# Seven block products for eight on all 2048 output columns in two quarters of an MLP, with four of the products moved into the first projection

## The chip, the cores and the metric

The kernel runs on one core of a Trainium2 chip. The metric is device microseconds per execution; lower is better. The kernel before takes 2056.1 us, the median of three runs (2055.78 to 2056.94).

The engines go by the profile's names: PE is TensorE (matmuls), PEld its weight loads, DVE is VectorE, ACT is ScalarE, POOL is GpSimd, and SP is the queue that issues nearly all DMAs.

## What is computed

One layer of a transformer trunk in float32 on 256 tokens of width 2048: a mixer of retention and gated DeltaNet, a cross-attention, a squared-ReLU MLP with a hidden width of 8192, and a final RMSNorm. The change touches the MLP alone:

```python
h = rms_norm(x, norm_ffn_g[l])
x = x + jnp.square(jax.nn.relu(h @ w_ff1[l])) @ w_ff2[l]
...
return rms_norm(x, norm_final_g)
```

`w_ff1` is 2048 x 8192 and `w_ff2` is 8192 x 2048. Both are read from HBM once.

## The kernel before

**Products of split operands.** Every float32 operand of a matmul is split into a high part, rounded by a cast on ACT (`whi`, line 125), and the remainder, a subtraction on DVE (`wlo`, line 126). A product of two split matrices is three matmuls: high x high, high x low, low x high. Weights come in fetches of 1 MiB (`fetch`, line 104) into one of three `raw` buffers, and are split in two halves of 128 x 1024. The split halves lie in `whi`/`wlo` (three buffers each), and every fourth half in `whx`/`wlx` (`half_tiles`), so that four halves are alive at a time: the cast of a half can start when PE is done with the half four before it.

**The MLP** runs in four quarters (`fb`, line 1258), each of 2048 hidden columns.

- *First projection* of a quarter: eight calls of `blocks` (line 221), each 256 hidden columns, with the weights stationary. A block takes two fetches, that is four halves. It ends in PSUM in the `s0`/`s1` tiles; ACT copies one part out (line 217), DVE adds the other (218), and `evac_h` (line 1266) squares the ReLU on DVE (1267), casts the high part on ACT (1269) and subtracts the low part on DVE (1270) into the quads `hid`.
- *Second projection* of a quarter: 256 tokens x 2048 hidden rows times 2048 x 2048 of `w_ff2`. The output columns are four groups of 512, `n` = 0 to 3; the hidden rows are four quads of 512, `q` = 0 to 3. `plain(n, q)` (line 1187) fetches one 512 x 512 piece and does 24 matmuls (four rows of blocks, two token halves, three matmuls). `add` (line 1135) adds a finished PSUM tile into the result on DVE.

**Seven for eight.** Hidden rows 0 to 1023 of a quarter (`q` = 0, 1) times columns 0 to 1023 (`n` = 0, 1) are a product of 2 x 2 blocks: the tokens in halves, the hidden rows in even and odd strips of 128, the columns in two groups of 512. `with_seven` (line 1156) does it in the seven products of Strassen's scheme in Winograd's form. A `product` (line 1196) is one token half times one block: 12 matmuls. It casts and subtracts a block's halves (lines 1202 and 1203), and, where `then` is given, forms the next difference of blocks on DVE (1207, two subtractions of 128 x 1024). The four blocks `b11`, `b12`, `b22`, `b21` lie in `rt` and `tr`, a 1 MiB block in each half, loaded by `load_block` (line 1164). The sums of the token side are made on DVE and ACT during the first projection (`token_sums`, line 1146). Some products go into several output tiles, and so `add` reads one PSUM tile twice. The rest (`n` = 2, 3 in all rows, `n` = 0, 1 in the second half of the rows) is `plain`: 12 of these and seven products make a quarter's second projection.

**What sets the order.** The program is written as one stream; a scheduler then orders each engine's instructions by priority. Fetches, casts and splits have a high priority and run ahead as far as buffers let them. Two orders are pinned in the code: `triple` (line 1179) puts each matmul of the second projection after the last one of the step before (`ends`), and `add_later` (line 1141) puts an `add` after the last split that was recorded so far. PSUM has two pairs `s0`/`s1` and four banks `b`; `shared` and `p5` are two of the banks, and `shared` holds one product after another: a product that starts in it must wait until DVE has added the one before into the result.

Of the kernel before, what the change touches and what calls it, by code (L numbers as in the profile page):

```python
# [14 lines left out]
ALU = mybir.AluOpType  # L15
# [37 lines left out]
def trunk(ctx: ExitStack, tc: tile.TileContext, x_f, mem_f, positions, lead_f, small_f, w_in, ret_gn_g, w_out, w_xq,  # L53
# [41 lines left out]
    def step():  # L95
        if steps and next(steps[0], steps) is steps:
            steps.pop(0)
# [91 lines left out]
    def cols(w, c0, n=512):  # L189
        return lambda q: [(0, w[q * 512:(q + 1) * 512, c0:c0 + n])]  # L190

    def blocks_in_steps(quads, w, c0, nb, evac):

        k = 16 // nb
        ps = stream_ps()
        n = nb * P
        for g in range(KT // k):  # L200
            halves = fetch([(0, w[g * k * P:(g + 1) * k * P, c0:c0 + n])], k, n, at=AT_BLOCKS)
            for i in range(k):
                kk = g * k + i
                xh, xhl = quads[kk // 4][0][:, kk % 4, :], quads[kk // 4].both[:, kk % 4, :]
                wh, wl = halves[i // (k // 2)]
                for b in range(nb):
                    bs = slice(b * P, (b + 1) * P)
                    lh, ll = wh[:, i % (k // 2), bs], wl[:, i % (k // 2), bs]
                    pe.matmul(ps[b], lh, xhl, start=kk == 0, stop=False)  # L209
                    pe.matmul(ps[b][:, :S], ll, xh, start=False, stop=kk == KT - 1)  # L210
                if i % (k // 2) == k // 2 - 1:
                    step()
                    yield
        for b in range(nb):
            with tc.high_priority(offset=50000):
                o = sm.tile([P, S], F32, name="bo", tag="bo", bufs=2)
                act.activation(o, ps[b][:, S:], AF.Copy)  # L217
                vec.tensor_add(o, o, ps[b][:, :S])  # L218
                evac(b, o)
# [936 lines left out]
    def with_seven(hid, rows, last):  # L1156


        own = [stream_ps() for _ in range(2)]
        shared, p5 = bank(), bank()  # L1160
        own += [[bank(), bank()]] * 2
        opened, ends, reads = set(), [], []

        def load_block(to, which, n):

# [47 lines left out]
        def part(b, t):  # L1213
            return lambda i: [a[:, 2 * (i % 2) + b, t * P:(t + 1) * P] for a in hid[i // 2]]
# [1 line left out]
        def summed(j):  # L1216
            return lambda i: [a[:, i, j * P:(j + 1) * P] for a in s_hl]

        first = 2 if last else 3
        plain(first, 0)  # L1220
        load_block(b11, 0, 0)
        plain(first, 1)
        load_block(b12, 0, 1)
        product(shared, part(0, 0), b11, "shared", (b11, b12, b11))
        read((0, 0, shared))
        plain(first, 2)
        load_block(b22, 1, 1)
        product(p5, summed(0), b11, "p5", (b11, b22, b11))
        read((1, 0, p5), (1, 1, p5))
        plain(0, 2)  # L1230
        product(own[1][0], summed(3), b22, (1, 0), (b12, b22, b12))
        plain(first, 3)
        load_block(b21, 1, 0)
        read(*((first, t, own[first][t]) for t in range(NT)))
        product(shared, summed(1), b11, "shared", (b11, b21, b11))
        read((1, 0, shared))
        plain(0, 3)
        product(own[0][0], part(1, 0), b21, (0, 0))
        read((0, 0, own[0][0]))
        if not last:  # L1240
            plain(2, 0)
        plain(1, 2)
        product(shared, summed(2), b12, "shared")
        read((0, 1, shared), (1, 1, shared))
        if not last:
            plain(2, 1)
        product(own[0][1], part(1, 1), b11, (0, 1))
        read((0, 1, own[0][1]))
        if not last:
            plain(2, 2)  # L1250
            plain(2, 3)
            read(*((2, t, own[2][t]) for t in range(NT)))
        plain(1, 3)
        read(*((1, t, own[1][t]) for t in range(NT)))
        for those in reads:
            add(*those)

    for fb in range(4):
        hid = []
        rows = w_ff2[0, fb * D:(fb + 1) * D, :]  # L1260
        for b2 in range(8):
            hs = fp.tile([P, 2, S], F32, name="hs", tag="hs", bufs=2)
            if b2 % 2 == 0:
                hid.append(quad_a())

            def evac_h(b, ps):
                vec.scalar_tensor_tensor(hs[:, b, :], ps, 0.0, ps, op0=ALU.max, op1=ALU.mult)
                qh, ql = (a[:, b2 % 2 * 2 + b, :] for a in hid[-1])
                act.activation(qh, hs[:, b, :], AF.Copy)
                vec.tensor_sub(ql, hs[:, b, :], qh.bitcast(F32))  # L1270
# [97 lines left out]
```

## Time and profile before

| | |
|---|---|
| median of three runs | 2056.1 us |
| profiled execution, its own time | 2056.91 us |
| its span, first to last instruction | 2055.2 us |
| PE busy | 2043.9 us, 99% of the span |
| DVE busy | 1511.4 us, 74% |
| ACT busy | 1130.3 us, 55% |
| second quarter of the MLP: first projection | 1527.99 to 1616.17 us |
| second quarter of the MLP: second projection | 1616.17 to 1700.52 us |
| third quarter: first and second projection | from 1700.52 and from 1788.70 to 1873.06 us |

A group's line gives the source line, the engine, the operation, what it writes and reads, the shape and the count; behind the bar its busy time and the mean of one in ns; behind the second bar the idle time of its engine just before it and what ended most of it. A row of the timeline starts with the start and the duration in us. In a table by windows each engine has its busy time and, in brackets, its count of instructions.

### The profile page before, as it was taken

The numbers are of one execution on the slowest core, as the hardware profiler recorded it, in microseconds if no ns is written. First come the engines' busy times: TensorE is split into PE (matmuls) and PEld (weight loads), VectorE is DVE, ScalarE is ACT, GpSimd is POOL, SyncE is SP. The second block draws the span as 40 slices with busy tenths as digits, with TensorE's granted clock in tenths as the row PEclk, the third lists the DMA queues.
The fourth block names the chain that finished last, engine by engine and source line by source line (L and its number), as shares of the span: only waits on it lengthen the run. The fifth ranks groups of instructions, "written<-read, shape, count | busy, mean of one in ns | idle before, by whom it ended". The sixth has DMA issues, their size and how long they took to land.

```text
span 2055.2 us, 28469 instructions
## 1 busy us (share of the span) xinstructions
PE 2043.9 (99%) x10874; PEld 1759.8 (86%) x10874; DVE 1511.4 (74%) x2409; ACT 1130.3 (55%) x1827; POOL 36.4 (2%) x50
## 2 busy tenths in 40 slices
PE   9999999999999999999999999999999999999998
PEld 7888888988888888888888899888888888888887
DVE  5887788779667875888567665777867777686785
ACT  5665764575457555755455565655545445454554
POOL 0000000000000000000000000000000000000000
PEclk9999999999999999999999999999999999999999
DMA  9689556456555655555467665569556646736662
GB/s 327 204 258 299 183 185 198 155 189 202 178 168 186 200 180 165 191 190 172 164 216 232 189 188 159 182 180 263 196 184 187 243 154 195 266 124 196 221 217 104
DMA packets 329225, 405.24 MB, mean 197 GB/s; under 512 B 34928, under 2 KB 239360, under 8 KB 328960
## 3 DMA queue, kind: packets, MB, share of 16 engines
q1 hardware_dynamic: 328656, 402.74, 60.8%
q8 instruction: 85, 1.39, 0.3%
q10 hardware_dynamic: 432, 0.69, 0.1%
q14 instruction: 52, 0.43, 0.1%
HBM read 389.74 MB, written 11.55 MB: 195 GB/s over the span
## 4 chain that ended last, share of the span: by engine, by line
PE 96%; DVE 1%; DMA 1%; issue 1%; ACT 1%; SPq 0%; POOLq 0%; POOL 0%; DVEq 0%; ACTq 0%
PE s L209 33%; PE s L210 17%; PE b L1182 9%; PE s L167 8%; PE s L168 8%; PE s L166 8%; PE s L1182 5%; PE s L399 1%; PE s L398 1%; PE s L400 1%; PE b L793 1%; PE b L826 1%; PE b L138 0%; DMA raw<-w_ff 0%; PE b L137 0%
## 5 line engine op out<-in xcount | busy, mean ns | idle before, releaser
L126 DVE TENSOR_TENSOR wlo<-raw,whi 128x1024 fp32r<-128x1024 f32 x610 | 744.9, 1222 | 344.2 <-ACT whi L125 338.2
L209 PE MATMUL s<-q,whi 128*128 128x512 f32 x2816 | 975.0, 391 | 0.8 <-DVE bo L218 0.6
L125 ACT ACTIVATE whi<-raw 128x1024 fp32r<-128x1024 f32 x610 | 646.3, 1060 | 574.9 <-PE s L209 204.1
L210 PE MATMUL s<-q,wlo 128*128 128x256 f32 x2816 | 771.8, 281 | 0.4 <-DVE wlo L126 0.3
L209 PEld LDWEIGHTS s<-q,whi 128*128 128x128 f32 x2816 | 521.1, 188 | 105.0 <-DVE bo L218 0.9
L210 PEld LDWEIGHTS s<-q,wlo 128*128 128x128 f32 x2816 | 528.9, 188 | 11.5 <-DVE wlo L126 1.2
L167 PE MATMUL s<-wlo,q 128*128 128x512 f32 x716 | 281.7, 393 | 0.0
L168 PE MATMUL s<-whi,q 128*128 128x512 f32 x716 | 279.4, 390 | 0.0
L166 PE MATMUL s<-whi,q 128*128 128x512 f32 x716 | 258.9, 390 | 0.0
L166 PEld LDWEIGHTS s<-whi,q 128*128 128x128 f32 x716 | 134.3, 188 | 28.0
L168 PEld LDWEIGHTS s<-whi,q 128*128 128x128 f32 x716 | 134.6, 188 | 27.0
L167 PEld LDWEIGHTS s<-wlo,q 128*128 128x128 f32 x716 | 134.6, 188 | 26.7
L217 ACT ACTIVATE bo<-s 128x256 f32<-128x256 f32 x192 | 72.9, 380 | 108.2 <-PE s L210 108.1
L218 DVE TENSOR_TENSOR bo<-bo,s 128x256 f32<-128x256 f32 x192 | 79.9, 416 | 54.0 <-ACT bo L217 53.7
L1182 PE MATMUL b<-whi,q 128*128 128x512 f32 x360 | 114.7, 389 | 0.0
L209 PE MATMUL s<-q,whx 128*128 128x512 f32 x256 | 89.4, 389 | 0.0
L126 DVE TENSOR_TENSOR wlx<-raw,whx 128x1024 fp32r<-128x1024 f32 x54 | 66.0, 1222 | 28.1 <-ACT whx L125 27.2
L125 ACT ACTIVATE whx<-raw 128x1024 fp32r<-128x1024 f32 x54 | 57.2, 1060 | 52.5 <-PE s L209 23.0
L1182 PE MATMUL s<-whi,q 128*128 128x512 f32 x248 | 79.8, 389 | 0.0
L1182 PEld LDWEIGHTS b<-whi,q 128*128 128x128 f32 x360 | 67.6, 188 | 14.1
L210 PE MATMUL s<-q,wlx 128*128 128x256 f32 x256 | 71.2, 280 | 0.0
L1182 PE MATMUL b<-wlo,q 128*128 128x512 f32 x180 | 70.1, 389 | 0.0
(383 smaller groups left out, 2186.0 us busy)
## 6 DMA issues: line engine op xcount, KB each, us to landing
raw<-w_in SPq DMA_DIRECT2D x143, 1024.0 KB
raw<-w_ff SPq DMA_DIRECT2D x112, 1024.0 KB
raw<-w_xkv SPq DMA_DIRECT2D x29, 1024.0 KB
raw<-w_out SPq DMA_DIRECT2D x16, 1024.0 KB
raw<-w_xq SPq DMA_DIRECT2D x16, 1024.0 KB
raw<-w_xo SPq DMA_DIRECT2D x16, 1024.0 KB
rt<-w_ff SPq DMA_DIRECT2D x8, 1024.0 KB
tr<-w_ff SPq DMA_DIRECT2D x8, 1024.0 KB
```

Of the source, the lines that this page charges most:

```text
L125: latest["hi"] = act.activation(hi[:, cs], src[:, cs], AF.Copy).ins
L126: latest["lo"] = vec.tensor_sub(lo[:, cs], src[:, cs], hi[:, cs].bitcast(F32)).ins
L166: pe.matmul(o, xh, wh, start=first, stop=False)
L167: pe.matmul(o, xh, wl, start=False, stop=False)
L168: pe.matmul(o, xl, wh, start=False, stop=last)
L209: pe.matmul(ps[b], lh, xhl, start=kk == 0, stop=False)
L210: pe.matmul(ps[b][:, :S], ll, xh, start=False, stop=kk == KT - 1)
L217: act.activation(o, ps[b][:, S:], AF.Copy)
L218: vec.tensor_add(o, o, ps[b][:, :S])
L398: pe.matmul(o, xh, wh, start=kk == 0 and c0 == 0, stop=False)
L399: pe.matmul(o, xh, wl, start=False, stop=False)
L1182: ins = pe.matmul(o, lhs[l], rhs[r], start=key not in opened, stop=last and j == 2, skip_group_check=True).ins
```

## The change

The second and third quarter (`fb` 1 and 2, called *early* in the code) do the seven products on columns 1024 to 2047 as well, and begin with the first unit's products during the first projection. The first and the fourth quarter are as before.

- Per early quarter 8 `plain` and 14 products replace 12 `plain` and 7 products.
- `with_seven` becomes a generator. In an early quarter the first block is loaded after the fourth block of the first projection, and then after each of the last four of the eight blocks one product is done: `part(0, 0)`, `summed(0)`, `summed(1)`, `summed(2)`. The matmuls of the first projection are pinned behind these (`ends`).
- The other three products of the first unit, the 8 `plain` and the seven products of the second unit follow. The second unit's blocks are loaded into the same four places of `rt` and `tr` as these come free.
- In the last four blocks of an early quarter's first projection the squared ReLU is no longer one instruction on DVE but two on ACT (`Relu`, then `Square`).

```diff
@@ blocks_in_steps
-                    pe.matmul(ps[b], lh, xhl, start=kk == 0, stop=False)
-                    pe.matmul(ps[b][:, :S], ll, xh, start=False, stop=kk == KT - 1)
+                    with tc.issue_after(ends[-1]) if ends else ExitStack():
+                        pe.matmul(ps[b], lh, xhl, start=kk == 0, stop=False)
+                        ins = pe.matmul(ps[b][:, :S], ll, xh, start=False, stop=kk == KT - 1).ins
                 if i % (k // 2) == k // 2 - 1:
+                    if ends is not None:
+                        ends.append(ins)
@@ with_seven
+        if early:
+            load_block(b11, 0, 0)
+            yield
+            load_block(b12, 0, 1)
+            product(shared, part(0, 0), b11, "shared", (b11, b12, b11))
+            read((0, 0, shared))
+            yield
+            load_block(b22, 1, 1)
+            product(p5, summed(0), b11, "p5", (b11, b22, b11))
+            read((1, 0, p5), (1, 1, p5))
+            yield
+            load_block(b21, 1, 0)
+            product(shared, summed(1), b11, "shared", (b12, b22, b12))
+            read((1, 0, shared))
+            yield
+            product(shared, summed(2), b12, "shared", (b11, b21, b11))
+            read((0, 1, shared), (1, 1, shared))
+            yield
+            for n in range(2):
+                take(n, stream_ps())
+            plain(0, 2)
+            load_block(b12, 0, 3)
+            product(own[1][0], summed(3), b22, (1, 0))
+            plain(0, 3)
+            load_block(b22, 1, 3)
+            product(own[0][0], part(1, 0), b21, (0, 0))
+            read((0, 0, own[0][0]))
+            product(own[0][1], part(1, 1), b11, (0, 1))
+            read((0, 1, own[0][1]))
+            plain(1, 2)
+            load_block(b11, 0, 2)
+            take(2, [bank(), bank()])
+            plain(2, 2)
+            load_block(b21, 1, 2)
+            opened.difference_update(("shared", "p5"))
+            product(shared, part(0, 0), b11, "shared", (b11, b12, b11))
+            read((2, 0, shared))
+            plain(1, 3)
+            read(*((1, t, own[1][t]) for t in range(NT)))
+            product(p5, summed(0), b11, "p5", (b11, b22, b11))
+            read((3, 0, p5), (3, 1, p5))
+            plain(2, 3)
+            take(3, stream_ps())
+            product(own[3][0], summed(3), b22, (3, 0), (b12, b22, b12))
+            plain(3, 2)
+            product(shared, summed(1), b11, "shared", (b11, b21, b11))
+            read((3, 0, shared))
+            plain(3, 3)
+            read(*((3, t, own[3][t]) for t in range(NT)))
+            product(own[2][0], part(1, 0), b21, (2, 0))
+            read((2, 0, own[2][0]))
+            product(shared, summed(2), b12, "shared")
+            read((2, 1, shared), (3, 1, shared))
+            product(own[2][1], part(1, 1), b11, (2, 1))
+            read((2, 1, own[2][1]))
+        else:
...
@@ evac_h and the loop
+                if early and b2 > 3:
+                    act.activation(ps, ps, AF.Relu)
+                    act.activation(hs[:, b, :], ps, AF.Square)
+                else:
+                    vec.scalar_tensor_tensor(hs[:, b, :], ps, 0.0, ps, op0=ALU.max, op1=ALU.mult)
...
-            blocks(h3, w_ff1[0], fb * D + b2 * 256, 2, evac_h)
+            blocks(h3, w_ff1[0], fb * D + b2 * 256, 2, evac_h, ends if early else None)
+            if early and b2 > 2:
+                next(parts_of)
...
-        with_seven(hid, rows, fb == 3)
+        for _ in parts_of:
+            pass
```

Where the instructions stand after the scheduler shows in the built programs. The source lines shift: 218 becomes 221, 1138 becomes 1141, 1203 becomes 1206, 1207 becomes 1210, 1267 becomes 1341, 1269 becomes 1343, 1270 becomes 1344; 1338 and 1339 are the new ReLU and square. Names keep their buffer numbers here.

**DVE ahead of the end of the first projection's last block.** Before, in the second quarter, the splits of that block's second fetch (`raw_15223`) stand between the steps of the evacuation of the seventh block (`s0_15080`, `s1_15081`), and the splits of the first `plain` step (`raw_15285`) follow:

```order
L126 TENSOR_TENSOR wlo_15226<-raw_15223,whi_15225 128x1024
L218 TENSOR_TENSOR bo_15166<-bo_15166,s0_15080 128x256
L1267 SCALAR_TENSOR_TENSOR hs_15078<-bo_15166 128x256
L126 TENSOR_TENSOR wlo_15230<-raw_15223,whi_15229 128x1024
L218 TENSOR_TENSOR bo_15172<-bo_15172,s1_15081 128x256
L1270 TENSOR_TENSOR q_15079<-hs_15078,q_15079 128x256
L1267 SCALAR_TENSOR_TENSOR hs_15078<-bo_15172 128x256
L126 TENSOR_TENSOR wlo_15288<-raw_15285,whi_15287 128x1024
L1270 TENSOR_TENSOR q_15079<-hs_15078,q_15079 128x256
L126 TENSOR_TENSOR wlx_15292<-raw_15285,whx_15291 128x1024
```

Now, in the same quarter, the splits of the last block's second fetch (`raw_15304`) are followed by the end of the seventh block's evacuation, the splits of the fourth product (`whi_15360`, `whi_15364`), two differences of blocks, and the addition of `b_14879`, the `shared` bank with the third product in it, into which the fourth product is to go:

```order
L126 TENSOR_TENSOR wlo_15307<-raw_15304,whi_15306 128x1024
L126 TENSOR_TENSOR wlx_15311<-raw_15304,whx_15310 128x1024
L1344 TENSOR_TENSOR q_15133<-hs_15132,q_15133 128x256 x2
L1206 TENSOR_TENSOR wlo_15361<-rt_10152,whi_15360 128x1024
L1206 TENSOR_TENSOR wlo_15365<-rt_10152,whi_15364 128x1024
L1210 TENSOR_TENSOR rt_10152<-tr_13007,rt_10152 128x1024 x2
L1141 SCALAR_TENSOR_TENSOR res_13006<-b_14879,rstd3q_13000,res_13006 128x512
L126 TENSOR_TENSOR wlo_15390<-raw_15387,whi_15389 128x1024
```

The square of the ReLU has left DVE here, and a product's two splits, two differences and one addition have come in; the addition stands behind the differences.

**DVE in the second projection, where a difference is formed.** Before, in the second quarter, one product with its differences is followed by a fetched step (`raw_15552`) and two additions of one finished `plain` column group:

```order
L1203 TENSOR_TENSOR wlo_15529<-rt_10152,whi_15528 128x1024
L1203 TENSOR_TENSOR wlx_15533<-rt_10152,whx_15532 128x1024
L1207 TENSOR_TENSOR rt_10152<-tr_13007,rt_10152 128x1024 x2
L126 TENSOR_TENSOR wlo_15555<-raw_15552,whi_15554 128x1024
L1138 SCALAR_TENSOR_TENSOR res_13006<-b_15283,rstd3q_13000,res_13006 128x512
L1138 SCALAR_TENSOR_TENSOR res_13006<-b_15284,rstd3q_13000,res_13006 128x512
L126 TENSOR_TENSOR wlo_15559<-raw_15552,whi_15558 128x1024
```

Now, around the product `summed(3)` of the second unit (`whi_15712`, `whi_15716`), with `raw_15674` being `plain(2, 3)` and `raw_15734` being `plain(3, 2)`:

```order
L1141 SCALAR_TENSOR_TENSOR res_13006<-s0_15385,rstd3q_13000,res_13006 128x512
L1141 SCALAR_TENSOR_TENSOR res_13006<-s1_15386,rstd3q_13000,res_13006 128x512
L126 TENSOR_TENSOR wlx_15681<-raw_15674,whx_15680 128x1024
L1206 TENSOR_TENSOR wlo_15713<-tr_13007,whi_15712 128x1024
L1141 SCALAR_TENSOR_TENSOR res_13006<-b_14880,rstd3q_13000,res_13006 128x512 x2
L1206 TENSOR_TENSOR wlo_15717<-tr_13007,whi_15716 128x1024
L1210 TENSOR_TENSOR rt_10152<-tr_13007,rt_10152 128x1024 x2
L126 TENSOR_TENSOR wlo_15737<-raw_15734,whi_15736 128x1024
```

Four additions and two differences now stand between the splits of three steps.

**ACT at the evacuation of the seventh block.** Before, its PSUM tiles are copied out (`bo_15166`, `bo_15172`) between casts, and the high part of `q` is cast when DVE has squared:

```order
L217 ACTIVATE bo_15166<-s0_15080 128x256
L125 ACTIVATE whi_15229<-raw_15223 128x1024
L217 ACTIVATE bo_15172<-s1_15081 128x256
L1269 ACTIVATE q_15079<-hs_15078 128x256
L125 ACTIVATE whi_15287<-raw_15285 128x1024
L1269 ACTIVATE q_15079<-hs_15078 128x256
L125 ACTIVATE whx_15291<-raw_15285 128x1024
```

Now the same block (`bo_15220`, `bo_15227`):

```order
L220 ACTIVATE bo_15220<-s0_15134 128x256
L125 ACTIVATE whi_15268<-raw_15262 128x1024
L220 ACTIVATE bo_15227<-s1_15135 128x256
L125 ACTIVATE whi_15306<-raw_15304 128x1024
L1338 ACTIVATE bo_15220<-bo_15220 128x256
L125 ACTIVATE whx_15310<-raw_15304 128x1024
L1339 ACTIVATE hs_15132<-bo_15220 128x256
L1338 ACTIVATE bo_15227<-bo_15227 128x256
L1343 ACTIVATE q_15133<-hs_15132 128x256
L1339 ACTIVATE hs_15132<-bo_15227 128x256
L1343 ACTIVATE q_15133<-hs_15132 128x256
L1205 ACTIVATE whi_15360<-rt_10152 128x1024
```

Each ReLU waits for DVE's line 221 and stands in ACT's queue ahead of the cast of a later weight half (`whx_15310`).

More of the change, by code (lines that the diff above doesn't have):

```diff
@@ L1154, in token_sums, with with_seven @@
         split([a[:, i, :] for a in s_hl], sv.rearrange("p a s -> p (a s)"))
-    def with_seven(hid, rows, last):
-        own = [stream_ps() for _ in range(2)]
+    def with_seven(hid, rows, last, early):
+        own = {}
         shared, p5 = bank(), bank()
-        own += [[bank(), bank()]] * 2
-        opened, ends, reads = set(), [], []
+        opened, reads = set(), []
         def load_block(to, which, n):
@@ L1217, in summed @@
             return lambda i: [a[:, i, j * P:(j + 1) * P] for a in s_hl]
[L1219 to L1246, printed above, removed]
@@ L1255, in with_seven @@
         for those in reads:
             add(*those)
+    ends = []
     for fb in range(4):
@@ L1260, in trunk @@
         rows = w_ff2[0, fb * D:(fb + 1) * D, :]
+        early = fb in (1, 2)
+        parts_of = with_seven(hid, rows, fb == 3, early)
+        ends.clear()
         for b2 in range(8):
```

49 lines of the change are left out of this document (41 added, 8 removed).

## The prediction, on record before the run

> **What bounds the kernel now.** I read the page's busy times and its chain of work that ended last, then the MLP by windows, then what PE waited for there.
>
> ```profile
> PE 2043.9 (99%) x10874; PEld 1759.8 (86%) x10874; DVE 1511.4 (74%) x2409; ACT 1130.3 (55%) x1827; POOL 36.4 (2%) x50
> ...
> PE 96%; DVE 1%; DMA 1%; issue 1%; ACT 1%; SPq 0%; POOLq 0%; POOL 0%; DVEq 0%; ACTq 0%
> ```
> ```profile
> 1380.00:2015.00 635.00, 635.00 (x3261) 544.84 (x3260) 473.79 (x610) 322.65 (x406) 0.00 (x0) 1.00 0.64 204
> ```
> ```profile
> 1527.99:1616.17 88.18, 88.18 (x514) 78.16 (x512) 61.57 (x96) 44.34 (x65) 0.00 (x0) 1.00 0.71 228
> 1616.17:1700.52 84.35, 84.35 (x374) 69.82 (x373) 64.71 (x65) 41.38 (x42) 0.00 (x0) 1.00 0.49 161
> ```
> ```profile
> PE s L1182 <- DVE wlo L1203: 0.3, 1, 0.3
> PE s L1182 <- DVE wlo L126: 0.2, 1, 0.2
> ```
>
> The chain is PE for 96%. In the window from 1380 to 2015 us PE is busy for every one of 635.00 us, at a granted clock of 1.00; the two other windows are the second quarter's projections. The last rows are all the waits of PE from 1380 us to the end: two, both near the end. So here time is the number of matmuls times their spacing, as long as nobody makes PE wait; DVE (64.71 of 84.35 us) and ACT are hidden.
>
> **What is removed.** The count of the second projection's matmuls alone gives their spacing:
>
> ```profile
> 1616.17:1700.52 84.35, 84.35 (x372) 69.64 (x372) 1.00 0.49 161
> ```
>
> That is 84.35 / 372 = 0.2267 us. The order of the two programs has 1392 matmuls of line 1182 before and 1368 after (line 1185 there): 24 fewer, 12 per early quarter, or **24 x 0.2267 = 5.44 us**. The blocks of the first projection keep their 256 pairs of matmuls (88.18 / 8 = 11.02 us a block, 2.755 us for one of its four halves). Outside the two quarters the orders of all engines are the same. So the question is what of 5.44 us comes back as waits of PE.
>
> **What DVE and ACT get.** The costs:
>
> ```profile
> L126 DVE TENSOR_TENSOR wlo<-raw,whi 128x1024 fp32r<-128x1024 f32 x610 | 744.9, 1222 | 344.2 <-ACT whi L125 338.2 <-PE b L698 0.5
> L125 ACT ACTIVATE whi<-raw 128x1024 fp32r<-128x1024 f32 x610 | 646.3, 1060 | 574.9 <-PE s L209 204.1 <-PE s L168 171.0 <-PE b L1182 52.8
> L218 DVE TENSOR_TENSOR bo<-bo,s 128x256 f32<-128x256 f32 x192 | 79.9, 416 | 54.0 <-ACT bo L217 53.7
> L217 ACT ACTIVATE bo<-s 128x256 f32<-128x256 f32 x192 | 72.9, 380 | 108.2 <-PE s L210 108.1
> ...
> L1207 DVE TENSOR_TENSOR rt<-tr,rt 128x1024 f32<-128x1024 f32 x24 | 28.2, 1217 | 0.0
> L1138 DVE SCALAR_TENSOR_TENSOR res<-b,rstd3q,res 128x512 f32<-128x512 f32 (+1 forms) x39 | 27.5, 736 | 1.5 <-PE b L168 1.5
> L1267 DVE SCALAR_TENSOR_TENSOR hs<-bo 128x256 f32<-128x256 f32 x64 | 26.9, 421 | 1.1
> L1270 DVE TENSOR_TENSOR q<-hs,q 128x256 fp32r<-128x256 f32 x64 | 26.7, 418 | 0.0
> L1269 ACT ACTIVATE q<-hs 128x256 fp32r<-128x256 f32 x64 | 26.0, 407 | 2.8 <-DVE hs L1267 2.8
> ```
>
> Queued behind one another, DVE's instructions start closer than they last:
>
> ```profile
> 1639.03 1.40 DVE L1138 SCALAR_TENSOR_TENSOR res<-b,rstd3q,res 128x512 f32<-128x512 f32 x2
> 1640.35 1.22 DVE L1203 TENSOR_TENSOR wlx<-tr,whx 128x1024 fp32r<-128x1024 f32 x1
> 1641.48 2.35 DVE L1207 TENSOR_TENSOR rt<-tr,rt 128x1024 f32<-128x1024 f32 x2
> 1643.76 2.35 DVE L126 TENSOR_TENSOR wlo<-raw,whi 128x1024 fp32r<-128x1024 f32 x2
> 1646.05 1.23 DVE L1203 TENSOR_TENSOR wlo<-rt,whi 128x1024 fp32r<-128x1024 f32 x1
> ```
>
> So an addition takes 1.32 / 2 = 0.66 us, a difference 1.14, a split 1.14.
>
> A *round* (a block, then a product) gives PE 11.02 + 12 x 0.2267 = 13.74 us. DVE has six splits (6.84), two differences (2.28), up to two additions (1.32) and four small steps of 0.42 (1.68): 12.1 us. ACT has six casts (6.36), two copies (0.76), two casts of `q` (0.81) and four new steps, priced as that cast (1.63): 9.6 us. The rest of the second projection, 8 `plain` and 10 products, gives PE 8 x 5.44 + 10 x 2.72 = 70.7 us; DVE has 36 splits (41.0), 8 differences (9.1), 16 additions (10.6) and two small steps: 61.5 us. Both fit, at 88% and 87%, against 77% of the second projection now. What can fail is a single place. I follow the running sum there.
>
> ```profile
> 1610.66 0.39 PE L209 MATMUL s<-q,whi 128*128 128x512 f32 x1
> ...
> 1610.80 1.06 ACT L125 ACTIVATE whx<-raw 128x1024 fp32r<-128x1024 f32 x1 [1.40 <-PE s L209]
> ```
> ```profile
> 1611.90 1.23 DVE L126 TENSOR_TENSOR wlx<-raw,whx 128x1024 fp32r<-128x1024 f32 x1 [1.21 <-ACT whx L125]
> ```
> ```profile
> 2016.40 1.22 DVE L1203 TENSOR_TENSOR wlo<-rt,whi 128x1024 fp32r<-128x1024 f32 x1
> ...
> 2017.68 0.50 PE L1182 MATMUL s<-wlo,q 128*128 128x512 f32 x1 [0.27 <-DVE wlo L1203]
> ```
>
> PE leaves a half at 1610.66; its buffer's next cast starts 0.14 us later, the split 1.10 us after that. In the last pair PE starts 0.06 us after the split it waited for ends (2017.62), and its matmul takes 0.50 us for 0.39, so a wait costs some 0.11 us beside itself.
>
> *The fourth product (new wait on the bank `shared`).* It starts when the eighth block ends, and must wait for the addition of the third product, which stands on DVE behind the fourth product's second split and two differences. That split's buffer comes free when the block is half done, two halves or 5.51 us earlier. The chain: 0.14 + 1.10 + 1.14 + 2.28 + 0.74 (the addition) + 0.06 = 5.46 us. It fits by 0.05 us, less than I can tell. Behind this matmul stands all of PE. Nothing at best, some 0.2 us if it misses; I take 0.15 a quarter, **0.3 us**.
>
> *The plain step (3, 2).* From the first split of the second `p5` product, which waits for its cast 2.6 us after the product ahead of it has started, DVE has six splits, four differences and five additions before the first split of (3, 2) starts: 6.84 + 4.56 + 3.30 = 14.7 us; with that split it is ready at 2.6 + 14.7 + 1.2 = 18.5 us. PE needs it after three products and two plain steps, 19.0 us. Cover 0.5 us: cost nothing, or up to 0.9 if the sixteen instructions follow at their durations (0.08 us more each).
>
> *The three products in a row at the end* give PE 8.16 us, DVE six splits and four additions, 9.5 us; but two of the splits are done before PE arrives, and the splits come out at least 1.2 us ahead. Nothing.
>
> *Evacuation on ACT.* The square's two steps are needed by `plain(0, 3)`, which starts 10.9 us after the last block: hidden. Were ACT late, the cover gone would be a whole cast and split.
>
> *DMA.* A quarter still loads 16 MiB for each projection. Four blocks beside eight fetches in 70.7 us make 12.6 MB, 178 GB/s, and a round's 3 MiB in 13.74 us 229 GB/s, while a stretch before ran at
>
> ```profile
> 1598.50:1617.00 18.50, 18.50 (x108) 16.38 (x107) 11.22 (x16) 8.51 (x12) 0.00 (x0) 1.00 1.03 382
> ```
>
> without making PE wait. The reload that SP can issue last, of the second unit's `b11`, waits for the first unit's seventh product's splits; it has some 11 us until its own cast must be done. At 382 GB/s 1 MiB takes 2.7 us. Nothing.
>
> **The sum.** The profiled execution took 2056.91 us, 1.71 around its span of 2055.2. 2056.91 - 5.44 + 0.3 = 2051.8; the median of the runs is 0.8 lower, so **2051.0 us**.
>
> **The rivals.**
>
> *DVE's backlog reaches PE.* Against it: the five rows above, 10 us of DVE without a gap, and no wait of PE. For it: both waits at the end are for a split. If instructions follow at their durations, the fourth product waits 0.3, (3, 2) 0.8, each with 0.1 for the restart: 1.2 a quarter; with 0.06 us between them as well, some 2.0. That gives back 2.4 to 4.0: **2053.4 to 2055.0 us**. It decides from 0.05 us at the first place.
>
> *ACT's queue behind the new ReLU (slower).* The ReLU waits for DVE's line 221, and a weight half's cast stands behind it, whose split DVE needs for PE: two first-in-first-out engines in a loop. When the loop closes, a round loses a cast and a split, 1.06 + 1.22 = 2.28 us; in all eight rounds 18.2: **2069 us**; slower than before by over 0.2% from five of the eight. It needs line 221 to be late by over 5 us: by the sums DVE reaches it 2 us after a block's product starts, ACT passes the cast 4.5 us after, and PE needs the split at 11.0. The idle time of 53.7 us behind line 217 in 192 evacuations, 0.28 each, speaks against it.
>
> *The longer evacuation itself.* Two steps of 0.41 us on ACT stand for one of 0.42 on DVE. Were each on PE's path, the 16 evacuations would cost 16 x 0.4 = 6.5 us: **2057.5 us**. Against it stand the 10.9 us above. The rows make the two engines' steps alike, and DVE the fuller engine. The Trainium skill, ScalarE: Activation LUTs, section Rules for kernel authors, advises VectorE and not ScalarE for a ReLU. By that rule this part of the change loses time, up to the 6.5 us; the trace bears it out only where the steps are waited for. No table is loaded for the new steps: the two programs hold five loads each, one of which lasts
>
> ```profile
> L253 ACT ACT_TABLE_LOAD  x1: 1283/1283/1283, 1.2 to 1.2; - x1
> ```
>
> *The change doesn't do what it says.* Then PE's count would not fall; the order shows that it does. A chance remains that PE loses as much in the strict order of blocks and products: **2056 us**.
>
> **How the numbers follow.** A measurement tells about 0.2% from no change, 4.1 us: faster is under 2052.0. My forecast, with at most 1 us of waits, has 0.62; DVE's backlog 0.22, within 0.2%; the queue behind the ReLU 0.09, slower; the longer evacuation 0.05 and no effect 0.02, both within. So faster 0.62, same 0.29, slower 0.09. The range goes from no wait and a low run, 2050.3, to the end of the backlog, 2055.0, which holds the first two cases (0.84).
>
> **What would show it.** In the second and third quarter 360 matmuls of the second projection's kind each for 372, 0.227 us apart; PE busy throughout both but for a gap of 0.1 to 0.2 us ahead of each quarter's fourth product, released by DVE's addition. A gap at (3, 2) released by a split would be the backlog; gaps inside the blocks, released by a cast, ACT's queue. The forecast is wrong if the sum of PE's gaps in the two quarters is over 1.4 us.

## The result, and the profile after

The kernel with the change takes 2051.68 us (median, 2049.37 to 2052.57), the kernel before 2056.14 us beside it (2054.61 to 2056.95): a ratio of 0.9978, with a 95% interval of 0.9969 to 0.9987. That is 4.5 us less, 2.7 to 6.4 by the interval. The profiled execution of the changed kernel took 2050.97 us for a span of 2049.2.

Two more lines have moved: 209 and 210 in the blocks are now 210 and 211, and 1182 in the products is 1185.

The page of the changed kernel, its busy times and the shares of its chain:

```profile
PE 2038.1 (99%) x10850; PEld 1756.6 (86%) x10850; DVE 1542.9 (75%) x2433; ACT 1153.2 (56%) x1871; POOL 36.3 (2%) x50
...
PE 96%; DMA 1%; DVE 1%; issue 1%; ACT 1%; SPq 0%; POOLq 0%; POOL 0%; DVEq 0%; ACTq 0%
```

PE has 24 instructions fewer (10874 before), DVE 24 and ACT 44 more, and the chain is PE for 96% as before. All that PE waited for from 1380 us to the end of the changed kernel (line, releaser, us in total, times, longest):

```profile
PE s L1185 <- DVE wlo L1206: 0.2, 1, 0.2
PE s L1185 <- DVE wlo L126: 0.2, 1, 0.2
```

These are the same two waits near the end as before; the two changed quarters have none that the view counts. To compare them I take the stretch from the first block of the second quarter to the first product of the fourth. First before, then after (length; busy time of PE, PEld, DVE, ACT, POOL with instructions; granted clock; DMA share; GB/s):

```profile
1527.99:1961.23 433.24, 433.24 (x2281) 374.12 (x2280) 314.14 (x416) 215.79 (x277) 0.00 (x0) 1.00 0.62 202
```
```profile
1526.80:1955.26 428.46, 428.46 (x2258) 369.70 (x2256) 345.01 (x440) 238.34 (x321) 0.00 (x0) 1.00 0.63 204
...
1581.91:1623.33 41.42, 41.42 (x230) 36.05 (x229) 34.88 (x41) 26.28 (x43) 0.00 (x0) 1.00 0.58 191
```

The stretch is 4.78 us shorter; the forecast was 5.14, and 24 matmuls alone would be 5.44. (The last row is its first three rounds of a product and a block.) The rest of the difference between the two profiled executions, 5.94 - 4.78 = 1.16 us, lies outside the change: in the MLP's first block, the first matmul behind those of the norm starts at 1362.40 us in place of 1363.65, behind code that is the same. In the five profiles below that leave the code ahead of it alone, this matmul starts between 1362.71 and 1364.75 us. So whole executions can be compared only to a microsecond or two; stretches of the same code, as the runs below show, agree to a few hundredths.

The place that the prediction named, around the second quarter's fourth product:

```profile
1617.90 1.06 ACT L1205 ACTIVATE whi<-rt 128x1024 fp32r<-128x1024 f32 x1 [1.68 <-PE s L210]
...
1618.99 1.23 DVE L1206 TENSOR_TENSOR wlo<-rt,whi 128x1024 fp32r<-128x1024 f32 x1 [1.51 <-ACT whi L1205]
...
1620.14 2.35 DVE L1210 TENSOR_TENSOR rt<-tr,rt 128x1024 f32<-128x1024 f32 x2
...
1622.41 0.74 DVE L1141 SCALAR_TENSOR_TENSOR res<-b,rstd3q,res 128x512 f32<-128x512 f32 x1
...
1623.33 0.43 PE L1185 MATMUL b<-whi,sh 128*128 128x512 f32 x1
...
1623.61 0.40 PE L1185 MATMUL b<-wlo,sh 128*128 128x512 f32 x1
```

Cast, split, two differences and addition stand behind one another as in the forecast's chain, and the matmul starts 0.18 us after the addition. It lasts 0.43 us for 0.40, and the second one follows 0.28 us behind it, where 0.233 is usual at such a place: some 0.05 us are lost, too little for the list of waits.

### The profile page after: what moved, and what is told of

The parts are those of the page before. It is cut to its first block, busy times and chain, and to the rows that moved or that the text cites. A ratio compares the mean times of both kernels' runs of the same rounds, so it can differ in the third digit from the quotient of the medians.

```text
span 2049.2 us, 28493 instructions
## 1 busy us (share of the span) xinstructions
PE 2038.1 (99%) x10850; PEld 1756.6 (86%) x10850; DVE 1542.9 (75%) x2433; ACT 1153.2 (56%) x1871; POOL 36.3 (2%) x50
## 4 chain that ended last, share of the span: by engine, by line
PE 96%; DMA 1%; DVE 1%; issue 1%; ACT 1%; SPq 0%; POOLq 0%; POOL 0%; DVEq 0%; ACTq 0%
PE s L210 33%; PE s L211 17%; PE s L167 8%; PE s L168 8%; PE s L166 8%; PE b L1185 7%; PE s L1185 6%; PE s L401 1%; PE s L403 1%; PE s L402 1%; PE b L796 1%; PE b L829 1%; PE b L138 0%; DMA raw<-w_ff 0%; PE b L137 0%
## 5 line engine op out<-in xcount | busy, mean ns | idle before, releaser
L126 DVE TENSOR_TENSOR wlo<-raw,whi 128x1024 fp32r<-128x1024 f32 x592 | 722.6, 1222 | 294.9 <-ACT whi L125 288.5
L125 ACT ACTIVATE whi<-raw 128x1024 fp32r<-128x1024 f32 x592 | 627.4, 1060 | 518.9 <-PE s L210 189.2
L1185 PE MATMUL b<-whi,q 128*128 128x512 f32 x244 | 78.8, 389 | 0.0
L1206 DVE TENSOR_TENSOR wlo<-rt,whi 128x1024 fp32r<-128x1024 f32 x46 | 56.1, 1223 | 23.3 <-ACT whi L1205 22.5
L1205 ACT ACTIVATE whi<-rt 128x1024 fp32r<-128x1024 f32 x46 | 48.8, 1060 | 33.4 <-PE s L1185 15.3
```

Source lines behind the costliest of these rows:

```text
L125: latest["hi"] = act.activation(hi[:, cs], src[:, cs], AF.Copy).ins
L126: latest["lo"] = vec.tensor_sub(lo[:, cs], src[:, cs], hi[:, cs].bitcast(F32)).ins
L1185: ins = pe.matmul(o, lhs[l], rhs[r], start=key not in opened, stop=last and j == 2, skip_group_check=True).ins
L1205: latest["hi"] = act.activation(hi, raw[:, c:c + 1024], AF.Copy).ins
L1206: latest["lo"] = vec.tensor_sub(lo, raw[:, c:c + 1024], hi.bitcast(F32)).ins
```

## The experiments

The theory: the time of this stretch is the number of TensorE's matmuls; the early products stay hidden only because VectorE gets a block's time beside each of them; and the one place without slack is the fourth product's wait for the bank `shared`. The rivals: VectorE's backlog, the ScalarE step, and a placing that doesn't matter. "After" stands for the changed kernel, "the stretch" for the one above. The kernel before was measured again beside these runs, and their ratios are to that: it took 2056.78 us beside the first four, 2057.41 beside the next three and 2057.74 beside the last, up to 1.6 us more than beside the changed kernel. Their medians can therefore be compared with a forecast time only to within such an amount.

**One quarter alone.**

```diff
-        early = fb in (1, 2)
+        early = fb == 1
```

> Only the MLP's second quarter takes the new order (early for fb == 1). The stretch from the start of the second quarter's blocks to the start of the fourth quarter's second projection is 433.24 us before and 428.46 us after. Theory (time is the number of TensorE's matmuls, and each early quarter gives the same): 12 matmuls of 0.2267 us go and about 0.33 us comes back, so 433.24 - 2.39 = 430.85 us (430.6 to 431.1), and a time of about 2056.1 - 2.3 = 2053.8 us. Rival (VectorE's backlog is carried from one early quarter into the next, so that the second gives less than the first): more than half of the gain here, under 430.5 us. Rival (most of the 4.4 us between the medians lies outside the two quarters): the time is the same as before within 1 us though the stretch is shorter.

Measured: 2054.85 us median, ratio 0.9990 (0.9981 to 0.9999). The stretch:

```profile
1529.10:1959.92 430.82, 430.82 (x2269) 371.89 (x2268) 329.63 (x428) 227.06 (x299) 0.00 (x0) 1.00 0.63 203
```

430.82 us, 0.03 from the expectation: 2.42 us less than before, half of 4.78 to within 0.03. Nothing is carried from one quarter to the next, and the gain belongs to the quarters that were changed. The median was expected at 2053.8, 2.3 us less than before, and came out a microsecond higher, 1.9 us below the kernel before beside it; so the rival of an unchanged time is out as well.

**The squared ReLU back on VectorE.**

```diff
-                if early and b2 > 3:
+                if False:
```

> The squared ReLU of the last four blocks goes back to VectorE as one instruction (ScalarE's ReLU and Square go); all else is as after. Theory (VectorE has room in a round of block and product): a round's 12.1 us of VectorE become 12.1 + 0.84 = 12.9 of 13.74, TensorE stays busy, the stretch of 428.46 us changes by -0.1 to +0.4 us, the time is within 0.5 us of 2051.7. Rival (VectorE had to be unloaded): it falls behind at the fourth product, whose addition stands behind the two more steps; then up to 0.84 us a quarter, 1.7 us in all: stretch 430.1, time 2053.4. Rival (the step on ScalarE costs time on the path, as the Trainium skill's advice on a ReLU would have it): the stretch gets shorter by over 0.3 us.

Measured: 2053.26 us, ratio 0.9984 (0.9975 to 0.9993), an interval that overlaps that of after. The time is 1.6 us above the expected 2051.7 and not within 0.5 of it; the kernel before beside it was 0.6 higher too, and the rest does not lie where the edit is, as the stretch shows. The stretch, and in it the three rounds of product and block:

```profile
1528.26:1956.81 428.55, 428.55 (x2258) 369.67 (x2256) 349.31 (x456) 228.99 (x289) 0.00 (x0) 1.00 0.64 204
1583.37:1624.82 41.45, 41.45 (x231) 36.02 (x229) 36.45 (x47) 22.83 (x31) 0.00 (x0) 1.00 0.59 191
```

The stretch is 0.09 us longer than after, as the theory had it. In the three rounds DVE is busy for 36.45 us where it was 34.88, still 88% of 41.45, and PE loses no more than 0.05 us a quarter to it, at the fourth product. So this part of the change neither gained nor lost anything that counts: the two steps on ScalarE cost nothing, since PE waits for none of them, and VectorE had room for the step. The Trainium skill, ScalarE: Activation LUTs, section Rules for kernel authors, advises VectorE for a ReLU; following it here makes the stretch 0.09 us longer and not shorter. The page's reason is the speed per element, given for bf16; how long the instruction lasts isn't on the path here.

**All products late.**

```diff
-            if early and b2 > 2:
-                next(parts_of)
```

> All 14 products of the second and third quarter are done after the first projection (no product between the blocks); TensorE has the same matmuls as after. Theory (the four early products are between the blocks because VectorE can't feed four in a row): they need 8 splits (9.1 us), 8 differences (9.1) and 4 additions (2.6), some 21 us of VectorE against 10.9 us of TensorE, less what VectorE does ahead of them: TensorE waits 5 to 9 us a quarter, the stretch is 438 to 446 us, the time 2061 to 2070 us, slower than before. The blocks, no longer alternated, fall back from 11.05 to 11.02 us. Rival (TensorE's count alone sets the time and the placing is needless): stretch 427.8 to 428.5 us, time 2051 to 2052.

Measured: 2078.35 us, ratio 1.0106 (1.0090 to 1.0121): slower than before by some 22 us, and far above the expected 2061 to 2070. What PE waited for from 1527 to 1720 us:

```profile
PE b L1185 <- DVE res L1141: 9.2, 2, 8.7
PE b L1185 <- DVE wlo L1206: 0.6, 1, 0.6
```

The timeline of the first of these quarters, DVE's rows and then PE's:

```profile
1627.54 1.22 DVE L1206 TENSOR_TENSOR wlo<-rt,whi 128x1024 fp32r<-128x1024 f32 x1
1628.67 1.22 DVE L126 TENSOR_TENSOR wlx<-raw,whx 128x1024 fp32r<-128x1024 f32 x1
1629.81 1.22 DVE L1206 TENSOR_TENSOR wlo<-rt,whi 128x1024 fp32r<-128x1024 f32 x1
1630.94 2.36 DVE L1210 TENSOR_TENSOR rt<-tr,rt 128x1024 f32<-128x1024 f32 x2
1633.21 0.75 DVE L1141 SCALAR_TENSOR_TENSOR res<-b,rstd3q,res 128x512 f32<-128x512 f32 x1
```
```profile
1634.11 0.77 PE L1185 MATMUL b<-whi,sh 128*128 128x512 f32 x1 [8.65 <-DVE res L1141]
1634.67 0.63 PE L1185 MATMUL b<-wlo,sh 128*128 128x512 f32 x1
1635.10 0.63 PE L1185 MATMUL b<-whi,sl 128*128 128x512 f32 x1
...
1638.51 0.63 PE L1185 MATMUL b<-wlo,sh 128*128 128x512 f32 x1
```

The mechanism is the expected one. The fourth product's first matmul waits 8.65 us for the third product's addition, and DVE works without a pause on the splits and differences ahead of it. The waits come to 9.8 us a quarter, just over the 5 to 9 that I gave. But the stretch is 452.95 us, 24.5 more than after, and the waits are only 19.6 of that. The rest stands in PE's rows: behind the long wait the matmuls follow one another 0.427 us apart and not 0.227. Windows of the same kernel, the slow matmuls and then the eight blocks:

```profile
1634.11:1638.90 4.79, 4.79 (x11) 3.77 (x12) 1.75 (x2) 1.06 (x1) 0.00 (x0) 0.50 0.82 285
```
```profile
1527.20:1615.38 88.18, 88.18 (x514) 78.17 (x512) 61.41 (x92) 49.36 (x77) 0.00 (x0) 1.00 0.73 234
```

The granted clock is 0.50 for these 11 matmuls; at 0.20 us each they lose 2.2 us, and seven behind the third quarter's long wait lose 1.4 more. With the slow restarts behind each wait that makes up the missing 24.5 - 19.6 = 4.9 us. That is what my expectation lacked. The second row is the other half of this run: without products between them the eight blocks take 88.18 us, 11.02 each, exactly as before the change, where the blocks between products take 11.05 after.

**A longer chain at the fourth product.**

```diff
-            read((1, 0, shared))
+            read((1, 0, shared, 1))
...
-    def add_later(n, t, ps):
+    def add_later(n, t, ps, more=0):
         with tc.issue_after(latest["lo"]):
+            for _ in range(more):
+                sv = fp.tile([P, 4, P], F32, name="sv", tag="sv", bufs=1)
+                with tc.high_priority(offset=200000):
+                    vec.scalar_tensor_tensor(sv.rearrange("p a s -> p (a s)"), ps, rstd3q[:, t:t + 1],
+                                             res[:, t, n * 512:(n + 1) * 512], op0=ALU.mult, op1=ALU.add)
             add(n, t, ps)
```

> One more addition of the third early product's sum, into a scratch tile, stands on VectorE between the fourth product's second split and its two differences; nothing else is moved, and no matmul added. In the profile of after the fourth product's first matmul starts 0.05 us late, 0.18 us after VectorE's addition. Theory (the chain half of block, cast, split, differences, addition, matmul fits with no slack): the added instruction takes 0.66 us, so a gap of 0.66 to 0.9 us appears at this place in each of the two quarters and nowhere else, the stretch is 428.46 + 1.4 = 429.9 us (429.7 to 430.3). Rival (the 0.05 us is the price of a switch from block to product, and the chain has slack that the sum did not see): no gap, 428.4 to 428.6 us. Rival (VectorE is so full that the extra work comes back elsewhere): gaps at a split behind it, over 430.5 us.

Measured: 2053.68 us, ratio 0.9987 (0.9978 to 0.9997). The timeline around the second quarter's fourth product, and the stretch:

```profile
1620.90 0.75 DVE L1150 SCALAR_TENSOR_TENSOR sv<-b,rstd3q,res 128x512 f32<-128x512 f32 x1
...
1621.56 2.35 DVE L1215 TENSOR_TENSOR rt<-tr,rt 128x1024 f32<-128x1024 f32 x2
...
1623.83 0.74 DVE L1141 SCALAR_TENSOR_TENSOR res<-b,rstd3q,res 128x512 f32<-128x512 f32 x1
...
1624.72 0.47 PE L1190 MATMUL b<-whi,sh 128*128 128x512 f32 x1 [0.46 <-DVE res L1141]
...
1625.03 0.39 PE L1190 MATMUL b<-wlo,sh 128*128 128x512 f32 x1
```
```profile
1527.57:1957.34 429.77, 428.84 (x2257) 369.67 (x2256) 346.28 (x442) 238.63 (x321) 0.00 (x0) 1.00 0.63 204
```

The stretch is 1.31 us longer than after, 0.65 a quarter, for an instruction that takes 0.66. From the eighth block's first matmul (1613.05, and 1612.28 after) to the product's second matmul it is 11.98 us for 11.33. The wait of 0.5 us at the addition comes twice and nowhere else. So the chain has no slack: what is added to it is added to the time.

**The addition first.**

```diff
+                if now:
+                    read_now()
                 for c in range(0, 2048, 1024) if then else ():
...
-            product(shared, summed(2), b12, "shared", (b11, b21, b11))
+            product(shared, summed(2), b12, "shared", (b11, b21, b11), True)
```

> The addition of the third early product's sum stands on VectorE ahead of the fourth product's two differences instead of behind them; nothing else is moved. Theory (the 0.05 us at the fourth product is its wait for the bank): the chain gets 2.3 us of slack, the round before the fourth product comes from 11.05 us of block to 11.05 with its first matmul 0.23 us behind the last one of the block instead of 0.28, and the stretch from 428.46 to 428.36 us (428.3 to 428.4); the 0.06 us that each of the other rounds takes beyond the sum stays. Rival (all of the 0.66 us is the price of switching between the two kinds of matmul): 428.46 us. No difference of the medians is to be seen: 2051.5 us.

Measured: 2052.73 us, ratio 0.9978 (0.9969 to 0.9987). The stretch, and the place:

```profile
1527.05:1955.39 428.34, 428.34 (x2258) 369.70 (x2256) 344.79 (x440) 238.42 (x321) 0.00 (x0) 1.00 0.63 204
```
```profile
1620.39 0.75 DVE L1141 SCALAR_TENSOR_TENSOR res<-b,rstd3q,res 128x512 f32<-128x512 f32 x1
...
1621.05 2.35 DVE L1212 TENSOR_TENSOR rt<-tr,rt 128x1024 f32<-128x1024 f32 x2
...
1623.58 0.40 PE L1185 MATMUL b<-whi,sh 128*128 128x512 f32 x1
...
1623.82 0.40 PE L1185 MATMUL b<-wlo,sh 128*128 128x512 f32 x1
```

The second matmul comes 0.24 us behind the first where it was 0.28, and the stretch is 0.12 us shorter. The 0.05 us were the wait for the bank; the other 0.55 us of what came back stay, and belong to something else. As expected no median shows this: 2052.73 us is above the 2051.5 that was expected, by less than the kernel before was higher beside it (1.3 us).

**Three quarters, and two attempts to mend it.** The obvious next step is to give the first quarter the new order as well:

```diff
-        early = fb in (1, 2)
+        early = fb < 3
...
-            if fb == 0:
-                place(b2)
+            if fb == 0 and b2 < 4:
+                place(2 * b2)
+                place(2 * b2 + 1)
```

> The first quarter of the MLP takes the new order too (early for fb < 3); so that the blocks b22 and b21, which are halves of the tile tr, come free in time, the step place is done twice in each of the first four blocks of the first quarter instead of once in each of its eight. Theory (each early quarter saves the same): the first quarter (from its first block to the next quarter's) takes 164.40 us after; 12 matmuls of 0.2267 us go, 0.33 us comes back: 162.0 us (161.7 to 162.4), and a time of about 2049.3 us. Rival (the work of place, pressed into half the blocks, or the products beside it make TensorE wait there): at least 1 us of gaps in the first four blocks, 163 us or more, no gain beyond after.

Measured: 2063.25 us, ratio 1.0032 (1.0019 to 1.0044): slower than before. The same with the addition first:

> Both edits: the first quarter takes the new order too, and the addition stands ahead of the differences in all three. Theory: the first quarter some 161.9 us, the other two 428.36 us, a time of about 2049.2 us, against some 2051.6 of the kernel after and 2056 of before. Rival (as in the run on the first quarter alone): its gain is eaten by waits in the first four blocks, 2051 to 2052 us.

Measured: 2063.93 us, ratio 1.0035 (1.0021 to 1.0049). The theory is wrong for this quarter in both, and the rivals are right that PE waits there; but the 2051 to 2052 us of the second is 12 us too low. The second projection of this quarter is as good as in the others (from the fourth product at 1465.17 to the next quarter's block at 1539.20 it takes the same 74.03 us); the loss is in the blocks. From ScalarE's first copy (line 220) for the last block ahead of the MLP to the fourth product it takes 110.88 us in the first of the two (1354.29 to 1465.17). In after it is 89.85 from the same copy to the end of the eight blocks (1352.59 to 1442.44), and three products of 2.76 would make it 98.1. So some 12.7 us are lost. PE's waits from 1355 to 1465 us in the first of the two kernels, DVE's work at their start, and a window behind the longest:

```profile
PE s L211 <- DVE wlx L126: 4.7, 1, 4.7
PE s L211 <- DVE wlo L126: 3.2, 3, 1.7
PE s L210 <- ACT whx L125: 1.7, 1, 1.7
```
```profile
1363.32 4.61 DVE L1123 STREAM_TRANSPOSE tr<-rt 128x1024 f32<-128x1024 f32 x4
1367.86 1.18 DVE L126 TENSOR_TENSOR wlo<-raw,whi 128x1024 fp32r<-128x1024 f32 x1
...
1369.03 1.22 DVE L126 TENSOR_TENSOR wlx<-raw,whx 128x1024 fp32r<-128x1024 f32 x1
```
```profile
1370.30:1374.70 4.40, 4.40 (x14) 3.82 (x15) 0.00 (x0) 0.36 (x1) 0.00 (x0) 0.50 0.83 156
```

The waits make 9.6 us of the loss, and half of the 4.40 us at a clock of 0.50, 2.2 us, is lost as well. The four transposes that make `tr`, 4.61 us on DVE, stand ahead of two splits, one for the second block and behind it the one (`wlx`) for the last half of the first block, for which PE waits 4.7 us. In after the first of the two is done ahead of the transposes; but the split for the last half stands behind them there too, at 1367.98, and PE does not wait for it. What differs is PE's own order. First DVE and PE in after, then PE in the run with three quarters:

```profile
1363.44 4.61 DVE L1123 STREAM_TRANSPOSE tr<-rt 128x1024 f32<-128x1024 f32 x4
1367.98 1.18 DVE L126 TENSOR_TENSOR wlx<-raw,whx 128x1024 fp32r<-128x1024 f32 x1
```
```profile
1366.94 0.63 PE L210 MATMUL s<-q,whx 128*128 128x512 f32 x2
```
```profile
1364.89 0.73 PE L210 MATMUL s<-q,whx 128*128 128x512 f32 x2 [1.69 <-ACT whx L125]
...
1370.30 0.80 PE L211 MATMUL s<-q,wlx 128*128 128x256 f32 x2 [4.68 <-DVE wlx L126]
```

The new order pins the matmuls of each half behind those of the half before (`ends`), so PE comes to the first block's last half right behind the norm's matmuls. In after nothing pins the first quarter's blocks, and in the built program the scheduler has put three halves of the second block ahead of most of the first block's last half. No run has the first quarter early without the pins, so how much of the loss is theirs and how much the transposes' is not shown. In later blocks there are three waits more for splits (3.2 us in all). A last version moves the transposes behind the first block's splits and spreads `place` by halves of `tr`:

```diff
-    for c in range(4):
-        vec.transpose(*(a[:, 4 * c:4 * c + 4, :].rearrange("p k s -> p (k s)") for a in (tr, rt)))
...
+            if fb == b2 == 0:
+                for c in range(4):
+                    with tc.issue_after(splits[-1]):
+                        vec.transpose(*(a[:, 4 * c:4 * c + 4, :].rearrange("p k s -> p (k s)") for a in (tr, rt)))
+            if fb == 0:
+                for j in range((0, 2, 4, 6, 8, 11, 14, 16)[b2], (2, 4, 6, 8, 11, 14, 16, 16)[b2]):
+                    place(j % 8, j // 8 * 8)
```

> As the run with both edits (new order in the first three quarters, addition ahead of the differences), but the work that made TensorE wait in the first quarter's blocks is put otherwise: the four transposes that make tr stand on VectorE behind the splits of the first block and not ahead of two of them, and place is done in halves of eight row groups (k), two halves in each of the first four blocks, three in the fifth and sixth, two in the seventh, so that b22 (the first eight groups) comes free first. Theory (the first quarter lost 13 us only by what stood ahead of the splits and loads, not by its products): no wait over 1 us in the first quarter, 162 to 163 us for it, a time of 2049 to 2050.5 us. Rival (the DMAs of place, 128 bytes a packet, and three loads a round don't fit beside each other): gaps of 1 to 2 us at splits in the fourth to seventh block, 3 to 6 us in all, 2052 to 2056 us.

Measured: 2061.00 us, ratio 1.0016 (1.0007 to 1.0025). The waits from 1355 to 1470 us:

```profile
PE s L214 <- DVE wlo L128: 2.1, 4, 0.8
PE s L213 <- ACT whi L127: 1.8, 1, 1.8
PE s L213 <- ACT whx L127: 1.7, 1, 1.7
PE s L214 <- DVE wlx L128: 0.8, 1, 0.8
```

The theory is wrong again. The wait of 4.7 us is gone, but seven are left, 6.4 us in all, and the same stretch still takes 109.03 us (1354.11 to 1463.14), 10.9 more than 98.1. All but 2.5 us of the waits lie behind the first early product; they come to 3.9 us, 1.8 of it for a cast and the rest for splits, which is within the rival's 3 to 6; its time of 2052 to 2056 us is missed all the same, since the waits at the first block and matmuls at half the clock behind two pairs of waits come on top. That the packets of `place` delay the loads, as the rival has it, is not tested by a run. At the longest of these waits the trace speaks for it: the cast that PE waits for starts at 1440.12 us, when ScalarE has waited 5.83 us for the load, and SP issued that load at 1432.34, 7.8 us earlier, right behind eight transfers of `place`. The wait of 1.7 us for the cast of the first block's last half is in all three kernels with an early first quarter, as the pins would have it. The cast itself is not late: in the run with three quarters it starts 9.51 us behind the copy named above (1363.80), and 9.99 in after (1362.58). No kernel of this study beats the changed one by more than the 0.1 us that the addition put first saves in the stretch.

## Why the prediction was right

- *The matmuls.* 24 fewer, at 0.2267 us each, as reckoned; the run with one quarter shows half of it, 2.42 us of 4.78.
- *The fourth product.* The place, the releaser and the order on DVE are as reckoned. I had the chain fit by 0.05 us and allowed 0.15 for it; it misses by 0.05. The one term that was off is the last: 0.18 us from the addition's end to the matmul, and 0.15 in the run with the longer chain, where the matmul does wait for it, for the 0.06 that I took from a split. The two runs on the chain show that there is no slack, and that this is a wait for the bank.
- *The plain step (3, 2).* I reckoned a cover of 0.5 us. In after its first split and its first matmul are:

```profile
1673.41 1.22 DVE L126 TENSOR_TENSOR wlo<-raw,whi 128x1024 fp32r<-128x1024 f32 x1
```
```profile
1675.10 0.62 PE L1185 MATMUL s<-whi,q 128*128 128x512 f32 x2
```

  The split ends at 1674.63, 0.47 us ahead. The sum of sixteen steps held because the spacing of queued instructions (1.14, 0.66) was read from the timeline and not their lengths (1.22, 0.74): from the first of them at 1658.76 to this split it is 14.65 us for the 14.7 reckoned.
- *DVE and ACT in a round.* Reckoned 12.1 and 9.6 us of 13.74; measured 34.88 / 3 = 11.6 and 26.28 / 3 = 8.8 of 13.81. No backlog, and no loop between ACT and DVE. (The five rows that I called 10 us of DVE without a gap span 8.2, from 1639.03 to 1647.28; no term of the sum hangs on it.)
- *The evacuation on ACT.* Hidden, as reckoned; the run with the square on DVE shows it from the other side.
- *The term that was mis-sized*: what comes back. I priced 0.3 us, all of it at the fourth product; 0.66 us came back, and only 0.1 of it there. A round takes 41.42 / 3 = 13.81 us for the 13.74 that I added up from a block and a product apart, 0.06 more, 0.4 in the six full rounds; the last 0.15 stand at the other joints. The sum took the pitch of a long run of equal matmuls for each piece, and a change of kind costs: the first product's first five matmuls start 0.229 to 0.236 us apart for 0.227, and the block behind it begins with two of 0.233. The run with all products late shows that the alternation is the cause of the blocks' part, since the same blocks without products between them take 11.02 us. Why a matmul is some 5 ns longer behind such a change stays open.
- *The time.* 2051.0 forecast, 2051.68 measured. The profiled run was forecast at 2051.8 and took 2050.97, but 1.16 us of its difference to before lie in unchanged code: by the stretch alone it would have been 2052.1. So the forecast was 0.4 us too low in what it could know. That the median lies below 2052.0, which I had set as the limit of "faster", is partly luck: it does so by 0.3 us, and four of the ten executions are above.

## What to carry to other kernels

Where one engine is busy without a gap, a change is worth its instructions times their pitch, and the work of the forecast is to follow the one chain that ends latest, with the spacing of queued instructions and not their lengths; then add a few hundredths of a us for each joint at which kinds of work alternate. A placing that costs nothing may be needed all the same: with the four products behind the blocks, the same instructions made the kernel 1.1% slower than before, not 0.2% faster. And a good order does not carry over to a stage that has other work beside it: the order that made the second and third quarter 2.4 us shorter each made the first about 10 us longer, where transposes stand ahead of a split and pinned matmuls leave TensorE nothing else to do meanwhile.

## What the runs showed of the hardware

A wait of TensorE cost more than its length once it was some microseconds long. Behind the two waits of 8.7 us (all products late) and those of 4.7 us (the first two kernels with an early first quarter) the granted clock was 0.50 for another 3.0 to 5.8 us, and matmuls of 512 columns stood 0.427 us apart in place of 0.227; so 1.4 to 2.9 us each are lost that no list of waits shows. Behind single waits of 0.5 us (the longer chain) there was no such stretch, nor behind one of 1.7 us by itself (at 1426.87 in the run with three quarters). Two shorter ones close together were enough: in the last kernel these windows, one around waits of 1.7 and 0.8 us and one around 1.8 and 0.8, hold such matmuls beside others at the full clock:

```profile
1362.00:1373.00 11.00, 8.53 (x41) 7.06 (x40) 9.87 (x14) 4.06 (x6) 0.70 (x1) 0.84 0.73 205
...
1434.00:1448.00 14.00, 11.35 (x55) 9.54 (x56) 7.99 (x11) 7.20 (x13) 0.00 (x0) 0.88 0.82 187
```

The Trainium skill, TensorE: Matmul & The Clock Gate, section Part 1: The HAM clock gate, has the array at half its clock after an idle window of about 3.4 us, and 512-column matmuls then 426.7 ns apart. The spacing agrees with the 0.427 us here, and the long waits with the window; the two pairs come to some 2.5 us each only, with work between the waits, so a single idle stretch of that length was not needed in this case. It gives 215.7 ns for them at the full clock; here they stand 226.7 ns apart in a run of 372, and the measurement decides.
